# FFN by Strassen's products: operations behind a product spread over the next products, and one ring of PSUM banks for the up-projection

## The chip, the cores and the metric

The kernel runs on one core of a Trainium2 chip. The metric is the device time of one execution in microseconds (us), the median of several runs. The engines of the core are TensorE (PE, with its weight loads as PEld), VectorE (DVE), ScalarE (ACT), GpSimd (POOL) and SyncE (SP), which here only issues transfers. Each works through its own queue of instructions in order, and a wait at the head of a queue holds back everything behind it.

## The reference, cut to what matters

One layer of a decoder for a prompt of 2048 tokens and 8 samples of one token: a mixing part (a gated MLP group and an attention group), then the part that is changed here, a feed-forward network with a causal convolution over three tokens:

```python
def conv_ffn(x, conv_prev, g_ffn, w_up, w_conv, b_conv, w_down):
    h = rmsnorm(x, g_ffn)
    up = h @ w_up                        # 1024 -> 2 x 2816
    xp = jnp.concatenate([conv_prev, up], axis=1)
    c = b_conv
    for k in range(CONV_W):              # 3 taps over the tokens
        c = c + xp[:, k:k + T] * w_conv[k]
    gate, val = c[..., :D_FF], c[..., D_FF:]
    y = (jax.nn.silu(gate) * val) @ w_down
    return y, xp[:, -(CONV_W - 1):]
```

All of it is float32. A final rmsnorm over `x + y` gives the output.

## The kernel before, in words

Stages follow each other: projections, the gated MLP group, attention of the prompt, the output projection, and from about 1334 us on the FFN. Attention of the samples over their long cache is a generator (`sample_stream`); its steps are put between other matmuls by `fill(ns)`, which counts down the planned TensorE time, so they stand at fixed places of the order.

**Float32 matmuls.** Each operand is split into a high part (a rounded copy made by ACT) and a low part (the difference, made by POOL or DVE), and a product is three matmuls: high x high, high x low, low x high (`mm3`).

**The FFN.** Tokens go in four blocks of 512 (the last has 520 columns, samples included), each block in two halves of 256 (260). For every block, 22 units (`up`) follow, one for each group of 128 of the 2816 columns. A unit needs four results: gate and value, each for two halves of the tokens. It gets them with seven products instead of eight (Strassen's scheme), called P0 to P6 here, with the activations B11, T2, B21, T3, T1, T4, B22, in this order; the names stand in the rows as `up<-B11h` and so on. One product is 12 matmuls of 128x256. DVE adds the products up: `s` is a copy of P0 that ACT makes, `u` are partial sums, and gate first half = P2 + s, value first half = P5 + u, value second half = P4 + u, gate second half = P6 + u.

Behind each of the four results stands the convolution (`conv`): ACT puts the two last columns of the previous tokens in front (`up<-halo`), makes the third tap with the bias (`c<-up,gn`), and saves the new last columns (`halo<-up`); DVE adds two taps (`SCALAR_TENSOR_TENSOR c<-up,gn,c`). Then `glu`: ACT makes SiLU of the gate, DVE multiplies, ACT makes the high part (`gh`), DVE the low part (`gl`).

The down-projection goes in pairs of units: when both units of a pair have their `gh` and `gl`, eight pieces (six matmuls of 128x512 into a bank `d`, then an add of DVE to `y`) follow, spread over the next two units by the table `PIECES`. A unit has seven slots: slot j is product Pj and what follows it, `rest(j)`: loads, splits of weights, and the pieces of the table. In the last block a piece has two parts of 260 columns, and `late` (the final norm of the first three blocks) takes one step in each slot.

**Weights.** `split_w` makes the seven weight forms of a unit, one a slot, five products ahead, in six buffers `wu`: ACT the high part, POOL the low part. Forms 1, 4 and 6 come from two sums of DVE (`t<-vraw`, then `t<-t,graw`), made here at form 1. Forms 3 and 6 need a subtraction of POOL each, made at form 3. `vraw` is loaded in three buffers; the load of the half that the next unit's sums read waits until POOL is done with form 3 of the present one. The queue of SP issues these loads and the samples' cache pages (`cn`, `ct`) in one order. `split_d` makes the parts of the down weights (`wdh`, `wdl`).

**PSUM.** The products use single banks by name: "a" for P0 and P2, "b" for P1, P3 and P5, "c" for P4, "e" for P6; two banks `d` for the pieces. All of a unit's post-processing is put into the queues right behind the product that it belongs to:

```python
            copy(s1, prod(0, "a"))
            rest(0)
            dve.tensor_add(u2, s1, prod(1, "b"))
            rest(1)
            p = prod(2, "a")
            ...
            p = prod(6, "e")
            dve.tensor_add(p, u2, p)
            cg = conv(b, fi, 0, ps["e"], hm, hm)
            last = glu(cg, cv, gt, hm, hm)
            next(last)
            if not (b == NB - 1 and fi == NF - 1):
                run(last)
            rest(6)
```

At the end of a block `ending` computes the last pair's down-projection; `last_pieces` does so for the last block and overlaps it with the final norm.

Of the kernel before, what the change touches and what calls it, by code (L numbers as in the profile page):

```python
# [38 lines left out]
TA = 7  # L39
# [12 lines left out]
def build(tc, A):  # L52
# [1292 lines left out]
    PIECES = ((0, 0, 1, 1, 1, 0, 0), (1, 1, 1, 1, 1, 0, 0))  # L1345
# [30 lines left out]

    def split_w():
# [7 lines left out]
        A21, A22 = VAL[2 * q], VAL[2 * q + 1]  # L1385
        if j == 0:
            src = A11
        elif j == 1:
            TMP[1] = sb.tile([128, 4, 128], F32, tag="t1", bufs=1, name="t1")
            TMP[2] = sb.tile([128, 4, 128], F32, tag="t2", bufs=1, name="t2")  # L1390
            dve.tensor_add(TMP[1], A21, A22)
            dve.tensor_sub(TMP[2], TMP[1], A11)  # L1392
            src = TMP[2]
        elif j == 2:
            src = A12
        elif j == 3:
            pool.tensor_sub(A21, A11, A21)
            pool.tensor_sub(TMP[2], A12, TMP[2])
            src = A21
        else:  # L1400
            src = (TMP[1], A22, TMP[2])[j - 4]
        wts[i] = form(src)
# [165 lines left out]
    with ExitStack() as Fx:  # L1568
        one = mkpool(Fx, "f_1", 1)
        sb = mkpool(Fx, "f_s", 2)  # L1570
        pu = mkpool(Fx, "f_pu", 1, PSUM)
# [164 lines left out]
        def conv(b, fi, gv, p, o, m):  # L1736
            npr = min(m, max(0, SEQ - BL[b][0] - o))
            ix = gv * NF + fi
            w = [g(W_CONV, j * 2 * NF + ix) for j in range(3)]
            c = sb.tile([128, 260], F32, tag=f"c{gv}", bufs=2, name=f"c{gv}")  # L1740
            act.activation(p[:, 0:2], halo[:, ix, :], AF.Copy)  # L1741
            act.activation(c[:, 0:m], p[:, 2:2 + m], AF.Identity, scale=w[2], bias=g(B_CONV, ix))  # L1742
            act.activation(halo[:, ix, :], p[:, npr:npr + 2], AF.Copy)  # L1743
            for j in (1, 0):
                dve.scalar_tensor_tensor(out=c[:, 0:npr], in0=p[:, j:j + npr], scalar=w[j], in1=c[:, 0:npr], op0=ALU.mult, op1=ALU.add)  # L1745
            if m > npr:
                act.activation(state[:, ix, 2, :], p[:, 2 + npr:2 + m], AF.Copy)
                for j in range(2):
                    dve.scalar_tensor_tensor(out=c[:, npr:m], in0=state[:, ix, j, :], scalar=w[j], in1=c[:, npr:m], op0=ALU.mult, op1=ALU.add)  # L1749
            return c  # L1750

        def glu(cg, cv, gt, o, m):
            act.activation(cg[:, 0:m], cg[:, 0:m], AF.Silu)  # L1753
            dve.tensor_mul(cv[:, 0:m], cg[:, 0:m], cv[:, 0:m])  # L1754
            yield
            split_to(gt[0][:, o:o + m], gt[1][:, o:o + m], cv[:, 0:m])
# [5 lines left out]
        def pieces(b, fi, gts):  # L1762
            for m in range(8):
                w = wd(b, fi, m)
                for o, nn in parts(b):
# [12 lines left out]
        BANKS = ("d", "ua", "d", "ub", "ue", "uc")  # L1778
# [5 lines left out]
        def ending(b, gts):  # L1784
            ps = {}

            def part(m, j):
                w, gt = wd(b, NF - 2, m)(j), gts[j]
                mm3(ps[m], [(*w, gt[0][:, 0:512], gt[1][:, 0:512])], j == 0, j == 1)
                fill(3 * 512 / 2.4)  # L1790

            for i in (0, 1, 2, 3, 4, 8, 9, 5, 10, 11, 12, 13, 6, 14, 7, 15):
                m = i % 8
                if i < 8:
                    ps[m] = bank(m)
                    part(m, 0)
                    continue
# [49 lines left out]
        def last_pieces(gts):  # L1847
# [8 lines left out]
            def part(i, j):  # L1856
                o, nn, m = todo[i]
                w, gt = wd(b, NF - 2, m)(j), gts[j]
                mm3(ps[i][:, 0:nn], [(*w, gt[0][:, o:o + nn], gt[1][:, o:o + nn])], j == 0, j == 1)

            for i in range(16 + LAG):
                if i < 16:
                    ps[i] = bank(i)
                    part(i, 0)
                if i >= LAG:
# [80 lines left out]

        def up(b, fi, it, side, slow, hs):
            hm, H, q = BL[b][1], h2[b], b * NF + fi
            odd, ps = fi % 2, {}

            def prod(j, name):
                w, (xh, xl) = wts.pop(7 * q + j), H[FORMS[j]]
                ps[name] = p = pu.tile([128, 512], F32, tag="u" + name, name="up")
# [5 lines left out]
            def rest(j):  # L1959
                todo, later[:] = later[:], []  # L1960
# [19 lines left out]
            dve.tensor_add(u3, u2, prod(3, "b"))  # L1980
            rest(3)
            p = prod(4, "c")
            dve.tensor_add(u2, u2, p)
            dve.tensor_add(p, u3, p)
            rest(4)
            p = prod(5, "b")
            dve.tensor_add(p, u3, p)  # L1987
            cv = conv(b, fi, 1, ps["b"], 0, hm)
            if odd:
                take(it, 99)  # L1990
            gt = [sb.tile([128, 520], F32R, tag=t, bufs=3, name=t) for t in ("gh", "gl")]
            run(glu(cg, cv, gt, 0, hm))
            cv = conv(b, fi, 1, ps["c"], hm, hm)
            rest(5)
            p = prod(6, "e")
            dve.tensor_add(p, u2, p)
            cg = conv(b, fi, 0, ps["e"], hm, hm)
            last = glu(cg, cv, gt, hm, hm)
            next(last)
            if not (b == NB - 1 and fi == NF - 1):  # L2000
                run(last)
            rest(6)
            return gt, last
# [33 lines left out]
        for b in range(NB):  # L2037
# [4 lines left out]
            for fi in range(NF):  # L2042
# [5 lines left out]
                gt, last = up(b, fi, it, side, slow if fi else none, hs)  # L2048
# [5 lines left out]
                if fi % 2 == 0:  # L2054
                    before = gt
                elif fi < NF - 1:
                    it = pieces(b, fi - 1, (before, gt))
            split_d()
            if b < NB - 1:
                it = ending(b, (before, gt))  # L2060
# [6 lines left out]
                continue  # L2067
            sp.dma_start(out=A["o_pconv"], in_=halo)
            sp.dma_start(out=A["o_sconv"][:, :, 0, :], in_=state[:, :, 1, :])
            sp.dma_start(out=A["o_sconv"][:, :, 1, :], in_=state[:, :, 2, :])  # L2070
            split_d()
            assert next(slow, 0) == 0
            it = last_pieces((before, gt))
# [121 lines left out]
```

## Time and profile before

| | us |
|---|---|
| median of 3 runs (3658.9 to 3668.77) | 3663.0 |
| the profiled execution | 3664.04 |
| its span, first to last instruction | 3662.3 |
| mean granted TensorE clock over the span | 0.907 |
| PE, PEld, DVE, ACT, POOL busy, share of the span | 83%, 72%, 58%, 44%, 48% |

The span is what the trace covers; the execution takes 1.7 us more. A busy share is a mean over all stages. What a stage is bound by is seen in the rows on what each engine waits for, and in the order of time.

### The profile page before, as it was taken

The numbers are of one execution on the slowest core, as the hardware profiler recorded it, in microseconds if no ns is written. First come the engines' busy times: TensorE is split into PE (matmuls) and PEld (weight loads), VectorE is DVE, ScalarE is ACT, GpSimd is POOL, SyncE is SP. The second block draws the span as 40 slices with busy tenths as digits, with TensorE's granted clock in tenths as the row PEclk, the third lists the DMA queues.
The fourth block names the chain that finished last, engine by engine and source line by source line (L and its number), as shares of the span: only waits on it lengthen the run. The fifth ranks groups of instructions, "written<-read, shape, count | busy, mean of one in ns | idle before, by whom it ended". The sixth has DMA issues, their size and how long they took to land. (4 is left out here: it accounts for less than half of the span.)

```text
span 3662.3 us, 71440 instructions
## 1 busy us (share of the span) xinstructions
PE 3040.3 (83%) x24340; PEld 2651.6 (72%) x24340; DVE 2120.6 (58%) x4367; ACT 1627.3 (44%) x4025; POOL 1770.5 (48%) x1665
## 2 busy tenths in 40 slices
PE   8998999999999967878778877777888885767676
PEld 7897887888778966767767776666676764767676
DVE  6564226777774455555565455566555556666565
ACT  4333336777872234433334344444344434444444
POOL 3332223223324555555555555556566655555554
PEclk9999999999999988989888898888999987878888
DMA  5448667887578965646666663476666533233232
GB/s 169 132 154 256 173 182 213 219 228 189 137 195 236 247 191 167 196 148 201 187 196 213 190 200 106 121 216 188 185 191 189 172 98 117 87 104 101 87 108 47
DMA packets 410760, 616.63 MB, mean 168 GB/s; under 512 B 69855, under 2 KB 300926, under 8 KB 410398
## 3 DMA queue, kind: packets, MB, share of 16 engines
q1 hardware_dynamic: 372560, 518.56, 47.8%
q0 software_dynamic: 26480, 87.14, 8.7%
q10 hardware_dynamic: 11358, 6.36, 0.6%
q8 instruction: 195, 3.19, 0.4%
q14 instruction: 167, 1.37, 0.1%
HBM read 547.58 MB, written 64.28 MB: 167 GB/s over the span
## 5 line engine op out<-in xcount | busy, mean ns | idle before, releaser
L126 POOL TENSOR_TENSOR wu<-t,wu 128x512 fp32r<-128x512 f32 x264 | 345.4, 1308 | 510.5 <-ACT wu L86 486.2
L1745 DVE SCALAR_TENSOR_TENSOR c<-up,gn,c 128x256 f32<-128x256 f32 (+2 forms) x704 | 340.7, 484 | 372.5 <-ACT halo L1743 359.9
L76 PE MATMUL up<-B21h,wu 128*128 128x256 f32 (+1 forms) x704 | 211.0, 376 | 366.5 <-ACT s L86 366.5
L76 PEld LDWEIGHTS up<-B21h,wu 128*128 128x128 f32 x704 | 165.2, 270 | 390.1 <-ACT s L86 386.7
L76 PE MATMUL dp<-gh,wdh 128*128 128x512 f32 (+1 forms) x800 | 305.4, 382 | 70.4 <-DVE y L1769 69.9
L126 POOL TENSOR_TENSOR wdl<-draw,wdh 128x512 fp32r<-128x512 f32 x171 | 228.6, 1337 | 254.9 <-ACT wdh L86 249.3
L86 ACT ACTIVATE wu<-t 128x512 fp32r<-128x512 f32 x264 | 164.1, 622 | 358.0 <-DVE t L1392 355.2
L76 PE MATMUL dp<-gl,wdh 128*128 128x512 f32 (+1 forms) x800 | 299.4, 374 | 0.0
L76 PE MATMUL dp<-gh,wdl 128*128 128x512 f32 (+1 forms) x800 | 297.2, 371 | 0.0
L126 POOL TENSOR_TENSOR wu<-vraw,wu 128x512 fp32r<-128x512 f32 x176 | 229.8, 1306 | 116.5 <-ACT wu L86 116.5
L126 POOL TENSOR_TENSOR wu<-graw,wu 128x512 fp32r<-128x512 f32 x176 | 228.2, 1297 | 103.6 <-ACT wu L86 103.6
L1741 ACT ACTIVATE up<-halo 128x2 f32<-128x2 f32 x352 | 59.3, 169 | 477.2 <-DVE up L1987 217.1
L1769 DVE TENSOR_TENSOR y<-y,dp 128x512 f32<-128x512 f32 (+1 forms) x400 | 226.6, 577 | 59.4 <-PE dp L76 58.5
L76 PE MATMUL s<-k,q 96*128 96x512 f32 (+2 forms) x960 | 254.1, 376 | 6.5 <-DVE S L1203 2.5
L76 PEld LDWEIGHTS dp<-gh,wdh 128*128 128x128 f32 x800 | 168.8, 211 | 88.7 <-DVE y L1769 74.0
L126 DVE TENSOR_TENSOR pl<-t,ph 128x512 fp32r<-128x512 f32 (+1 forms) x320 | 194.0, 606 | 53.0 <-ACT ph L86 49.4
L86 ACT ACTIVATE ph<-t 128x512 fp32r<-128x512 f32 (+1 forms) x320 | 170.2, 532 | 107.1 <-PE t L1227 102.8
L1215 ACT ACTIVATE S<-S,nm 128x512 f32<-128x512 f32 (+2 forms) x320 | 207.9, 650 | 5.7 <-POOL nm L1207 5.7
L1742 ACT ACTIVATE c<-up,gn 128x256 f32<-128x256 f32 (+1 forms) x352 | 199.3, 566 | 11.7
L76 PEld LDWEIGHTS s<-k,q 96*128 96x128 f32 x960 | 170.3, 192 | 45.2 <-DVE S L1203 10.1
L76 PEld LDWEIGHTS dp<-gh,wdl 128*128 128x128 f32 x800 | 166.5, 208 | 23.9
L76 PEld LDWEIGHTS dp<-gl,wdh 128*128 128x128 f32 x800 | 168.2, 210 | 11.7
(460 smaller groups left out, 9145.5 us busy)
## 6 DMA issues: line engine op xcount, KB each, us to landing
ct<-in_cT SPq DMA_DIRECT2D x1024, 144.0 KB
cn<-in_cN SPq DMA_DIRECT2D x1024, 128.0 KB
draw<-in_w_down SPq DMA_DIRECT2D x176, 256.0 KB
vraw<-in_w_up SPq DMA_DIRECT2D x174, 256.0 KB
graw<-in_w_up SPq DMA_DIRECT2D x87, 512.0 KB
q_sp<-qs SPq DMA_DIRECT2D x48, 256.0 KB
ft<-x_sp SPq DMA_DIRECT2D x48, 256.0 KB
xt<-in_xT SPq DMA_DIRECT2D x16, 512.0 KB
```

Of the source, the lines that this page charges most:

```text
L76: pe.matmul(out, lhsT=w, rhs=x, start=start, stop=stop)
L86: act.activation(out, in_, AF.Copy)
L126: (lo_eng or dve).tensor_sub(lo, src, f(hi))
L1215: act.activation(s, s, AF.Exp, scale=SCALE, bias=d["nm"][:, qb:qb + 1], accum_out=d["ls"][:, qb, r:r + 1])
L1741: act.activation(p[:, 0:2], halo[:, ix, :], AF.Copy)
L1742: act.activation(c[:, 0:m], p[:, 2:2 + m], AF.Identity, scale=w[2], bias=g(B_CONV, ix))
L1745: dve.scalar_tensor_tensor(out=c[:, 0:npr], in0=p[:, j:j + npr], scalar=w[j], in1=c[:, 0:npr], op0=ALU.mult, op1=ALU.add)
L1769: dve.tensor_add(y, y, p[:, 0:nn])
```

## The change

Five things change, all in the FFN. No operation is added or removed: every engine keeps its number of instructions.

- A table `defer` holds operations by slot, and `flush()` at the head of `rest` puts those of the present slot into the queues. The third tap and the halo copies (`conv_init`), the two taps of DVE (`taps`), SiLU, the product, `gh` and `gl` of one result now stand in different slots, up to slot 11 of the unit, that is slot 4 of the next one.
- The products' banks turn in one ring of four (`pu`, tag "u"); the bank of P5 is taken before that of P4.
- `PIECES` of the even unit is (0, 0, 0, 0, 1, 1, 1) and no longer (0, 0, 1, 1, 1, 0, 0).
- DVE's two sums for the weights are made one slot earlier (behind form 0), POOL's two subtractions too (behind form 2).
- `ending` and `last_pieces` call `flush()` for the operations that the last unit has left over, and the two stores of the convolution's state come four steps later.

```diff
-    PIECES = ((0, 0, 1, 1, 1, 0, 0), (1, 1, 1, 1, 1, 0, 0))
+    PIECES = ((0, 0, 0, 0, 1, 1, 1), (1, 1, 1, 1, 1, 0, 0))
...
+    def sums(A11, A21, A22):
+        for i in (1, 2):
+            TMP[i] = sb.tile([128, 4, 128], F32, tag=f"t{i}", bufs=1, name=f"t{i}")
+        dve.tensor_add(TMP[1], A21, A22)
+        dve.tensor_sub(TMP[2], TMP[1], A11)
...
+        wts[i] = form(src)
+        if j == 0 and not i:
+            return
         if j == 0:
...
+            sums(A11, A21, A22)
+        if j == 2:
             pool.tensor_sub(A21, A11, A21)
             pool.tensor_sub(TMP[2], A12, TMP[2])
...
-        pu = mkpool(Fx, "f_pu", 1, PSUM)
+        pu = mkpool(Fx, "f_pu", 4, PSUM)
...
+        def flush():
+            for fn in defer.pop(pos["t"], ()):
+                fn()
+            pos["t"] += 1
...
-            copy(s1, prod(0, "a"))
+            copy(s1, prod(0))
             rest(0)
-            dve.tensor_add(u2, s1, prod(1, "b"))
+            add(u2, s1, prod(1))
             rest(1)
-            p = prod(2, "a")
-            dve.tensor_add(p, s1, p)
-            cg = conv(b, fi, 0, ps["a"], 0, hm)
+            p = prod(2)
+            add(p, s1, p)
+            at_slot(2, lambda: init(0, 0, 2))
+            at_slot(3, lambda: tap(0, 0, 2))
             rest(2)
...
+            at_slot(5, lambda: silu(0), lambda: init(1, 0, 5))
+            at_slot(6, lambda: init(1, 1, 4), lambda: tap(1, 0, 5), lambda: tap(1, 1, 4))
+            rest(5)
+            p3 = prod(6)
+            at_slot(7, lambda: add(p3, u2, p3), lambda: init(0, 1, 6), lambda: gmul(0))
+            at_slot(8, lambda: ghi(0), lambda: tap(0, 1, 6))
+            at_slot(9, lambda: glo(0), lambda: silu(1))
+            at_slot(10, lambda: gmul(1), lambda: ghi(1))
+            at_slot(11, lambda: glo(1))
+            rest(6)
```

ACT's queue around the end of an odd unit in the second block, before. The first three rows belong to P6; `c<-c` is SiLU, `gh` the high part of the gated result, `wu` a weight form, and `s` the copy of the next unit's P0:

```order
L1741 ACTIVATE up<-halo 128x2
L1742 ACTIVATE c_26883<-up,gn 128x256
L1743 ACTIVATE halo<-up 128x2
L1753 ACTIVATE c_26883<-c_26883 128x256
L86 ACTIVATE gh<-c_26854 128x256
L86 ACTIVATE wu<-t_26785 128x512
L86 ACTIVATE s_26898<-up 128x256
L86 ACTIVATE wu<-vraw 128x512
```

The same place in the changed kernel:

```order
L1747 ACTIVATE up<-halo 128x2
L1748 ACTIVATE c_26869<-up,gn 128x256
L1749 ACTIVATE halo<-up 128x2
L86 ACTIVATE wu<-t_26754 128x512
L86 ACTIVATE s_26882<-up 128x256
L1747 ACTIVATE up<-halo 128x2
L1748 ACTIVATE c_26994<-up,gn 128x256
L1749 ACTIVATE halo<-up 128x2
L86 ACTIVATE wu<-vraw 128x512
L86 ACTIVATE gh<-c_26845 128x256
L86 ACTIVATE wu<-t_26755 128x512
L2010 ACTIVATE c_26994<-c_26994 128x256
```

SiLU (L1753, now L2010) and `gh` stood ahead of the copy `s` and now stand behind it; the halo copies of P6 stood ahead of it too and are now the rows right behind it.

DVE's queue in the even unit that follows, from P1's add to P4's, before (`t<-vraw` and `t<-t,graw` are the sums for the weights, `y` the add of a piece):

```order
L1974 TENSOR_TENSOR u_26899<-s_26898,up 128x256
L1977 TENSOR_TENSOR up<-s_26898,up 128x256
L1745 SCALAR_TENSOR_TENSOR c_27047<-up,gn,c_27047 128x256 x2
L1769 TENSOR_TENSOR y_26005<-y_26005,dp 128x512
L1980 TENSOR_TENSOR u_26900<-u_26899,up 128x256
L1391 TENSOR_TENSOR t_27080<-vraw 128x512
L1392 TENSOR_TENSOR t_27081<-t_27080,graw 128x512
L1769 TENSOR_TENSOR y_26007<-y_26007,dp 128x512
L1983 TENSOR_TENSOR u_26899<-u_26899,up 128x256
```

The same place in the changed kernel, up to the first piece's add:

```order
L2026 TENSOR_TENSOR u_26883<-s_26882,up 128x256
L1757 SCALAR_TENSOR_TENSOR c_26994<-up,gn,c_26994 128x256 x2
L2026 TENSOR_TENSOR up<-s_26882,up 128x256
L2023 TENSOR_TENSOR gl<-c_26845,gh 128x256
L1380 TENSOR_TENSOR t_27053<-vraw 128x512
L1381 TENSOR_TENSOR t_27054<-t_27053,graw 128x512
L2026 TENSOR_TENSOR u_26884<-u_26883,up 128x256
L2014 TENSOR_TENSOR c_26869<-c_26994,c_26869 128x256
L1757 SCALAR_TENSOR_TENSOR c_27044<-up,gn,c_27044 128x256 x2
L2026 TENSOR_TENSOR u_26883<-u_26883,up 128x256
L2026 TENSOR_TENSOR up<-u_26884,up 128x256
L2023 TENSOR_TENSOR gl<-c_26869,gh 128x256
```

The sums stood behind the add of P3 and now stand ahead of it, behind the add of P2; the rest of the previous unit's gate and product (taps, `gl`, `c<-c,c`, the second `gl`) stands among this unit's adds, and no piece comes before P4.

## Rows read from the trace of the kernel before

**Rows 1.** The page: busy shares, and the granted clock in 40 slices.
```profile
PE 3040.3 (83%) x24340; PEld 2651.6 (72%) x24340; DVE 2120.6 (58%) x4367; ACT 1627.3 (44%) x4025; POOL 1770.5 (48%) x1665
PEclk9999999999999988989888898888999987878888
```

**Rows 2.** Stretches (units 2 to 19): length; PE, PEld, DVE, ACT, POOL busy; clock; DMA; GB/s.
```profile
1392.00:1837.00 445.00, 364.32 (x3208) 319.02 (x3208) 234.69 (x479) 178.06 (x484) 252.80 (x200) 0.90 0.61 182
1961.00:2408.00 447.00, 358.98 (x3164) 318.40 (x3163) 237.64 (x491) 187.86 (x496) 250.39 (x199) 0.89 0.55 162
2529.00:2953.00 424.00, 354.09 (x2714) 298.62 (x2712) 236.94 (x456) 178.94 (x489) 254.69 (x205) 0.92 0.60 176
3093.00:3575.00 482.00, 334.01 (x2390) 325.25 (x2389) 297.65 (x643) 204.66 (x540) 272.07 (x208) 0.83 0.30 97
```

**Rows 3.** TensorE's waits from 1334 to 3640: total us, times, longest.
```profile
PE up L76 <- ACT s L86: 366.5, 73, 11.7
PE dp L76 <- DVE y L1769: 69.9, 20, 7.6
```

**Rows 4.** TensorE in time, an even unit: start, us, operation, idle time before.
```profile
2633.58 0.58 PE L76 MATMUL up<-B21h,wu 128*128 128x256 f32 x1 [7.54 <-ACT s L86]
...
2638.01 0.40 PE L76 MATMUL dp<-gl,wdh 128*128 128x512 f32 x1
```

**Rows 5.** ACT in time, the same stretch.
```profile
2628.98 0.63 ACT L86 ACTIVATE wu<-vraw 128x512 fp32r<-128x512 f32 x1 [2.60 <-POOL vraw L1397]
2629.52 0.16 ACT L1741 ACTIVATE up<-halo 128x2 f32<-128x2 f32 x1
...
2632.32 0.42 ACT L86 ACTIVATE gh<-c 128x256 fp32r<-128x256 f32 x1 [0.49 <-DVE c L1754]
2633.16 0.36 ACT L86 ACTIVATE s<-up 128x256 f32<-128x256 f32 x1
```

**Rows 6.** TensorE in time at full clock: P0, a piece, P1, a sample step.
```profile
2649.00 0.28 PE L76 MATMUL up<-B11h,wu 128*128 128x256 f32 x1
...
2650.42 0.40 PE L76 MATMUL dp<-gh,wdh 128*128 128x512 f32 x1
...
2651.80 0.28 PE L76 MATMUL up<-T2h,wu 128*128 128x256 f32 x1
...
2657.30 0.38 PE L76 MATMUL up<-B21h,wu 128*128 128x256 f32 x1 [0.41 <-ACT s L86]
```

**Rows 7.** Sample steps of TensorE (tile po), busy us in the third block.
```profile
2529.00:2953.00 424.00, 42.09 (x704) 17.09 (x704) 1.92 (x4) 0.92 0.60 176
```

**Rows 8.** DVE in time: an add and the taps behind it, and two prices of the sums.
```profile
2647.78 0.43 DVE L1987 TENSOR_TENSOR up<-u,up 128x256 f32<-128x256 f32 x1 [0.74 <-PE up L76]
2649.11 1.01 DVE L1745 SCALAR_TENSOR_TENSOR c<-up,gn,c 128x256 f32<-128x256 f32 x2 [0.90 <-ACT halo L1743]
...
2662.26 1.65 DVE L1391 TENSOR_TENSOR t<-vraw 128x512 f32<-128x512 f32 x1
2663.99 1.60 DVE L1392 TENSOR_TENSOR t<-t,graw 128x512 f32<-128x512 f32 x1
```

**Rows 9.** DVE by form in the second block: busy, mean ns, idle before.
```profile
L1391 DVE TENSOR_TENSOR t<-vraw 128x512 f32<-128x512 f32 x18 | 16.5, 918 | 11.8 <-DMA vraw<-in_w_up 9.0 <-POOL wdl L126 2.9
L1392 DVE TENSOR_TENSOR t<-t,graw 128x512 f32<-128x512 f32 x18 | 14.3, 795 | 1.6
```

**Rows 10.** The page: the low parts that POOL makes.
```profile
L126 POOL TENSOR_TENSOR wu<-t,wu 128x512 fp32r<-128x512 f32 x264 | 345.4, 1308 | 510.5 <-ACT wu L86 486.2
```

**Rows 11.** SP's queue in time: page loads of the samples, weight loads.
```profile
2216.58 9.33 SPq L66 DMA_DIRECT2D cn<-in_cN  x16
...
2226.48 0.86 SPq L66 DMA_DIRECT2D vraw<-in_w_up  x2
```

**Rows 12.** DVE in time, behind those loads.
```profile
2230.44 0.69 DVE L1391 TENSOR_TENSOR t<-vraw 128x512 f32<-128x512 f32 x1 [2.48 <-DMA vraw<-in_w_up]
```

**Rows 13.** The same view: units 0 and 1 of the second block.
```profile
1925.00:1962.00 37.00, 29.21 (x314) 27.96 (x315) 20.52 (x39) 16.01 (x41) 23.80 (x19) 0.87 0.76 246
```

More of the change, by code (lines that the diff above doesn't have):

```diff
@@ L1385, in split_w @@
         A21, A22 = VAL[2 * q], VAL[2 * q + 1]
-        if j == 0:
[L1387 to L1396, printed above, removed]
+        if j in (0, 2):
+            src = (A11, A12)[j // 2]
+        elif j == 1:
+            if not q:
+                sums(A11, A21, A22)
+            src = TMP[2]
+        else:
+            src = (A21, TMP[1], A22, TMP[2])[j - 3]
+        wts[i] = form(src)
+        if j == 0 and not i:
+            return
+        if j == 0:
+            sums(A11, A21, A22)
+        if j == 2:
             pool.tensor_sub(A21, A11, A21)
             pool.tensor_sub(TMP[2], A12, TMP[2])
[L1399 to L1402, printed above, removed]
         if j == 4:
@@ L1764, in pieces @@
                 w = wd(b, fi, m)
+                if m == 0:
+                    gts = [G[i] for i in gts]
                 for o, nn in parts(b):
@@ L1973, in up, with ghi, glo, add @@
+            def ghi(h):
+                if not h:
+                    G[q] = [sb.tile([128, 520], F32R, tag=t, bufs=3, name=t) for t in ("gh", "gl")]
+                copy(G[q][0][:, h * hm:h * hm + hm], c[1, h][:, 0:hm])
+            def glo(h):
+                o = slice(h * hm, h * hm + hm)
+                dve.tensor_sub(G[q][1][:, o], c[1, h][:, 0:hm], f(G[q][0][:, o]))
+            def add(out, a, p):
+                dve.tensor_add(out, a, p)
+            copy(s1, prod(0))
             rest(0)
-            dve.tensor_add(u2, s1, prod(1, "b"))
+            add(u2, s1, prod(1))
@@ L1985, in up @@
+            add(u2, u2, p)
+            add(p, u3, p)
             rest(4)
-            p = prod(5, "b")
-            dve.tensor_add(p, u3, p)
-            cv = conv(b, fi, 1, ps["b"], 0, hm)
+            p = prod(5)
+            add(p, u3, p)
+            at_slot(5, lambda: silu(0), lambda: init(1, 0, 5))
[3 more added lines that the diff above has]
+            at_slot(7, lambda: add(p3, u2, p3), lambda: init(0, 1, 6), lambda: gmul(0))
@@ L1996, in up @@
[L1996 to L2003, printed above, removed]
         def last_stat():
@@ L2047, in build @@
                     hs = load_h2(b + 1)
-                gt, last = up(b, fi, it, side, slow if fi else none, hs)
+                up(b, fi, it, side, slow if fi else none, hs)
                 if b == 0 and fi == 0:
@@ L2053, in build @@
                     take(load_y(b), 99)
[L2054 to L2057, printed above, removed]
+                last2 = b * NF + fi - 1, b * NF + fi
+                if fi % 2:
+                    it = pieces(b, fi - 1, last2) if fi < NF - 1 else none
             split_d()
             if b < NB - 1:
-                it = ending(b, (before, gt))
+                it = ending(b, last2)
                 for _ in range(8):
@@ L2067, in build @@
                 continue
+            split_d()
+            assert next(slow, 0) == 0
+            it = last_pieces(last2)
+            act.activation(sb.tile([128, 1], F32, tag="tw", bufs=1, name="tw"), epst, AF.Sqrt)
+            take(it, 4)
             sp.dma_start(out=A["o_pconv"], in_=halo)
@@ L2070, in build @@
             sp.dma_start(out=A["o_sconv"][:, :, 1, :], in_=state[:, :, 2, :])
-            split_d()
-            assert next(slow, 0) == 0
-            it = last_pieces((before, gt))
-            act.activation(sb.tile([128, 1], F32, tag="tw", bufs=1, name="tw"), epst, AF.Sqrt)
-            take(it, int(T6))
-            run(last)
-            take(it, int(TA))
+            take(it, int(T6) + int(TA) - 4)
             r0 = root(0)
```

72 lines of the change are left out of this document (44 added, 28 removed).

## The prediction, written before the changed kernel ran

> **What bounds the kernel now.** The page first: TensorE is busy 83% of the span, and its granted clock falls in the second half [rows 1]. Then the busy times by stretch, for the FFN: in units 2 to 19 of a block (nine pairs of units) TensorE is busy 364 of 445, 359 of 447, 354 of 424 and 334 of 482 us, and no other engine comes near its limit, POOL with 250 to 272 us and DVE with 235 to 298 [rows 2]. So an order of waits bounds it. TensorE's own waits name it: 366.5 us in 73 waits for ACT's copy `s`, and 69.9 us for DVE's adds of pieces [rows 3].
>
> How such a wait comes about stands in time. TensorE stops for 7.54 us before P2 of an even unit and then runs at 1.2 GHz until about 2638.0 [rows 4]. P2 goes into the bank that P0 left, and P0 waits there for the copy `s`. ACT makes it last: it is held 2.60 us by POOL's subtraction for a weight form, then come the halo copies, SiLU and `gh` of the unit before, each waiting for DVE, and `s` starts only at 2633.16 [rows 5]. At full clock TensorE needs far less: a product takes 1.42 us (2649.00 to 2650.42), a piece 1.38 (2650.42 to 2651.80) [rows 6]. A pair of units is 14 products and 8 pieces, 19.9 + 11.0 = 30.9 us; sample steps add 42.1 / 9 = 4.7 [rows 7]: 35.6 us, against (445 + 447 + 424) / 27 = 48.7 now. In the last block it is 31.6 (260 columns, no samples), against 482 / 9 = 53.6.
>
> **The change, part by part.** Counts stay, so everything is a matter of waits.
>
> *The copy `s` and the ring.* `s` no longer stands behind SiLU and `gh`, and P2 takes a bank that P4 left. The 7.5 us wait goes. What is late next? I go through an even unit of the changed kernel, from t = 0, the end of P5 of the odd unit before; until P4 of the even unit no piece stands in TensorE's way, so alone it would end P6 at 1.4, P0 at 2.8, P1 at 4.3, P2 at 5.7. The taps of P5 start 1.35 us after its end (add at 2647.78, taps at 2649.11) and take 1.0 [rows 8]. ACT then has two weight copies (0.54 from start to start [rows 5]), to 2.4, and the halo copies of P4 (0.85, what the 1.35 leave beside the add), to 3.25; DVE takes its taps to 4.3, then P6's add to 4.75, ACT P6's halo copies to 5.6, DVE P6's taps to 6.7. P3 needs that bank: 1.0 us late.
>
> *The sums a slot earlier.* They can't start before `vraw` has landed, and that load waits for POOL's low part of form 3. Its copy on ACT comes behind P5's halo copies and a down weight, at about 2.4, and POOL does the down weight and the form one after the other at 1.3 us each [rows 10], to about 4.5. From issue to use the one measured wait gives 3.1 us (issued by 2227.34, sums at 2230.44) [rows 11, 12]; with the issue 0.4: 8.1. The two sums cost 0.92 + 0.80 = 1.7 [rows 9], to 9.8. Behind them in DVE's queue stand P3's add, the product, two taps, P4's two adds and the second `gl`: five operations of 0.43 and a pair of taps of 1.0 [rows 8], 3.2, so `gl` is there at 13.0. The first piece stands behind P4, which ends at 9.6 with the 1.0 above; four of its matmuls (0.9) need nothing new, the fifth needs `gl`: 13.0 − 10.5 = 2.5 us wait. So an even unit still waits 1.0 + 2.5 = 3.5 us.
>
> *What comes on top or off.* A sample step stands in such a run more often than not and covers part: −0.9 (bounds 0 and −1.9). SP's queue: 16 page loads hold the weight loads 9.33 us [rows 11], and a load so held lands late by up to that; today 11.8 + 1.6 = 13.4 us of idle time at these sums in 18 units are all it costs [rows 9], since the sums come a slot later. Bounds 0 and 9.3 for an even unit; I take 1.6, since only some units are hit and most hits are short. An idle stretch can bring half speed: after 0.41 us none (a full-speed row, 0.38) [rows 6], after 7.54 us 4.4 us of it, a loss of 2.2 [rows 4]; for 2 to 4 us I take 1.7. Odd units have a piece behind each of five products and so twice the time for the same chains; bounds 0 and 3, I take 1.0. The pair: 35.6 + 3.5 − 0.9 + 1.6 + 1.7 + 1.0 = 42.5 us, and 27 x (48.7 − 42.5) = 167 us gained in three blocks.
>
> The rows of DVE show the sums at 0.69 us [rows 12] and at 1.65 and 1.60 us [rows 8]. The Trainium skill (GPSIMD Engine Reference, "Key points", and SBUF — State Buffer, "SBUF: two separate sides") says that GpSimd and a DVE operation with two SBUF inputs take one shared port in turn, each for a whole instruction. By that rule a POOL that works closer to the sums, as it will, makes the dear price the usual one: 3.25 for 1.7, and over 36 even units some 56 us less gained, 3411 us. The slow rows agree with it; the means of rows 9 lie between, and the sum goes by these.
>
> *The last block.* There DVE is busy 298 us in nine pairs, 33.1 a pair [rows 2], more than TensorE's 31.6, because of the final norm of the earlier blocks. DVE keeps waits that the change does not touch (0.9 us before each of the eight pairs of taps [rows 8], in part filled): 33.1 + 9 = 42 (bounds 36 and 50). Gain: 9 x (53.6 − 42) = 104 us.
>
> *Units without pieces* (0 and 1 of each block) take 37 us now [rows 13]. TensorE needs 2 x 9.9, POOL 2 x 9 x 1.3 = 23.4; with 6 us for the start of a block 29.5: 4 x 7 = 28 us. Unit 20 and the products of 21: 3 us in each block, 12. The end of a block keeps its work, with the leftovers in its queues: 0 (bounds −8 and 8 each). POOL's two subtractions a slot earlier free ACT of its 2.60 us wait, which is inside the above.
>
> The sum: 167 + 104 + 28 + 12 = 311, and 3664 − 311 = 3353; the profiled execution is 1 us above the median of three, so I say **3355 us**.
>
> **The rivals.** *Nearly all idle time goes* (14%): loads land in time and sample steps cover the rest. For it: no engine but TensorE has more to do in a pair than POOL's 254.7 / 9 = 28.3 us [rows 2]. Against it: the chain through `vraw` above. Pairs of 38 and 36 us: 27 x 10.7 + 9 x 17.6 + 28 + 20 = 495, 3169 us.
>
> *The sums at the head of DVE's queue take the place of the copy* (17%). Both units of a pair wait for `vraw` or for POOL, and DVE holds taps and adds behind it. For it: the idle time of these sums already names `vraw` and POOL [rows 9]. Against it: odd units have twice the time. Pairs of 47 and 48: 27 x 1.7 + 9 x 5.6 = 96, 3568 us.
>
> *No gain that can be measured* (3%): the deferred operations run in the old order in effect, since each queue waits at the same products. The rows of the order speak against it.
>
> *Slower* (6%): the page loads. With pairs 15% shorter the 16-fold bursts stand ahead of the weight loads more often; if every even unit gets `vraw` a whole burst late, the pair is 35.6 + 3.5 + 9.3 + 2.2 + 1.0 = 51.6, and with the last block as now 27 x 2.9 = 78 more: 3742 us. It decides from a mean delay of about 6.5 us on. Against it: a longer pair gives the queue its time back.
>
> **How the numbers follow.** The forecast has 60%, with a range of its own of 3280 to 3440. With half of the first rival and most of the second, 3190 to 3570 holds eight times in ten. Faster by over 0.3% (about what a measurement of this kernel can tell from no change): 0.60 + 0.14 + 0.17 = 0.91; the same 0.03; slower 0.06.
>
> **What the profile after would show.** Right: the wait of products for `s` under 60 us in all; new waits of P3 for DVE's taps and of `dp` for `gl` in even units, 1 to 4 us each; sums that wait for `vraw` in most even units; a granted clock of 0.93 or more in units 2 to 19 of the first three blocks; DVE the engine next to its limit in the last. Wrong: products that wait for `wu` (the weights bound it), waits of sample matmuls for their pages, or odd units with waits as long as the even ones.

## The result, and the profile after

The changed kernel takes 3551.9 us (median of three runs, 3551.3 to 3557.0) against 3663.0; the ratio is 0.970, 95% interval 0.967 to 0.972. It is faster by 111 us; the forecast was 308 us, 3355. The page of the changed kernel, answering to [rows 1]:

```profile
PE 3040.0 (86%) x24340; PEld 2625.1 (74%) x24340; DVE 2178.8 (61%) x4367; ACT 1609.0 (45%) x4029; POOL 1792.2 (50%) x1665
PEclk9999999999999998889988898997898988889988
```

TensorE has the same work, and the clock still falls in the second half. ACT has four instructions more than before (4029 against 4025): four more loads of its function tables, 1.28 us each. Units 2 to 19 of the four blocks, changed kernel, columns as in [rows 2]:

```profile
1380.10:1821.90 441.80, 365.58 (x3207) 314.62 (x3206) 242.39 (x482) 173.60 (x481) 256.66 (x199) 0.90 0.62 184
1944.00:2380.60 436.60, 355.49 (x3159) 312.00 (x3158) 248.26 (x495) 185.86 (x499) 260.22 (x201) 0.90 0.54 162
2509.10:2938.00 428.90, 359.76 (x2711) 297.45 (x2709) 239.85 (x460) 175.53 (x490) 261.23 (x207) 0.91 0.60 174
3057.80:3467.60 409.80, 329.41 (x2384) 313.25 (x2384) 332.55 (x645) 197.91 (x541) 276.32 (x209) 0.89 0.35 114
```

The first three blocks, for which 167 us were forecast, gained 8 (445 + 447 + 424 to 442 + 437 + 429); the last gained 72 (482 to 410). By the starts of the first products in both traces, units 0 and 1 of the four blocks went from 168 to 183 us (lost 15), unit 20 from 126 to 113, unit 21 with the end of the block from 238 to 206 (gained 32), and the FFN starts 3 us earlier: 8 + 72 − 15 + 13 + 32 + 3 = 113, against 112 us between the spans.

TensorE's waits in the changed kernel from 1334 to 3540, answering to [rows 3] (total us, times, longest):

```profile
PE dp L76 <- ACT gh L86: 178.6, 42, 14.0
PE dp L76 <- DVE gl L2023: 84.2, 49, 3.8
PE up L76 <- DVE u L2026: 40.0, 15, 7.9
PE dp L76 <- DVE y L1775: 31.7, 26, 4.5
PE up L76 <- ACT s L86: 19.3, 18, 3.0
PE up L76 <- DVE c L1757: 14.7, 12, 3.7
...
PE lp L76 <- ACT wd L86: 0.7, 1, 0.7
```

The wait for `s` is gone, from 366.5 us to 19.3. In its place the first piece waits for `gh` and `gl`. DVE's waits at the weight sums, same stretch, say why:

```profile
DVE t L1380 <- DMA vraw<-in_w_up: 142.9, 24, 10.4
DVE t L1380 <- issue: 75.0, 15, 12.6
DVE t L1380 <- POOL wu L126: 8.4, 4, 3.0
```

The kernel before had 32.5, 9.8 and, on POOL, 2.9 us there. For a wait marked `issue` the trace shows no releaser; these go with the load, since they fall to 1.4 us when it is issued earlier (below). One even unit of the second block shows the whole chain. SP's queue in the changed kernel (start, us, operation):

```profile
1988.67 6.80 SPq L66 DMA_DIRECT2D draw<-in_w_down  x3
1996.07 10.60 SPq L66 DMA_DIRECT2D ct<-in_cT  x16
...
2007.55 0.81 SPq L66 DMA_DIRECT2D vraw<-in_w_up  x2
```

POOL, in the same stretch, was done with the low part of form 3, for which the load waits, at 1996.3:

```profile
1995.04 1.27 POOL L126 TENSOR_TENSOR wu<-vraw,wu 128x512 fp32r<-128x512 f32 x1
```

The load's buffer was free at 1996.3, and the load went at 2007.5, behind sixteen pages of the samples. DVE, from the first `gl` on:

```profile
1999.33 0.42 DVE L2023 TENSOR_TENSOR gl<-c,gh 128x256 fp32r<-128x256 f32 x1
2012.38 0.69 DVE L1380 TENSOR_TENSOR t<-vraw 128x512 f32<-128x512 f32 x1 [12.64 <-issue]
2013.18 0.69 DVE L1381 TENSOR_TENSOR t<-t,graw 128x512 f32<-128x512 f32 x1
2013.79 0.42 DVE L2026 TENSOR_TENSOR u<-u,up 128x256 f32<-128x256 f32 x1
2014.12 0.42 DVE L2014 TENSOR_TENSOR c<-c,c 128x256 f32<-128x256 f32 x1
...
2016.03 1.11 DVE L2023 TENSOR_TENSOR gl<-c,gh 128x256 fp32r<-128x256 f32 x1
```

Behind the sums stand P3's add, the product `c` (from which ACT makes `gh`) and the second `gl`. TensorE, at the first piece:

```profile
2015.04 0.79 PE L76 MATMUL dp<-gh,wdh 128*128 128x512 f32 x1 [14.03 <-ACT gh L86]
2017.19 0.80 PE L76 MATMUL dp<-gl,wdh 128*128 128x512 f32 x1 [1.36 <-DVE gl L2023]
...
2021.62 0.57 PE L76 MATMUL dp<-gh,wdl 128*128 128x512 f32 x1
2022.03 0.39 PE L76 MATMUL dp<-gh,wdh 128*128 128x512 f32 x1
```

It stands for 14.03 us, and its matmuls then take 0.79 us in place of 0.39 (1.2 in place of 2.4 GHz; the granted clock from 2015 to 2022 is 0.50) until about 2022.0.

### The profile page after: what moved, and what is told of

Read it like the earlier page. It is cut to its first block, busy times and chain, and to the rows that moved or that the text cites. A ratio compares the mean times of both kernels' runs of the same rounds, so it can differ in the third digit from the quotient of the medians.

```text
span 3550.1 us, 71345 instructions
## 1 busy us (share of the span) xinstructions
PE 3040.0 (86%) x24340; PEld 2625.1 (74%) x24340; DVE 2178.8 (61%) x4367; ACT 1609.0 (45%) x4029; POOL 1792.2 (50%) x1665
## 5 line engine op out<-in xcount | busy, mean ns | idle before, releaser
L76 PE MATMUL dp<-gh,wdh 128*128 128x512 f32 (+1 forms) x800 | 306.4, 383 | 210.7 <-ACT gh L86 178.6
L126 POOL TENSOR_TENSOR wu<-t,wu 128x512 fp32r<-128x512 f32 x264 | 353.7, 1340 | 211.0 <-ACT wu L86 211.0
L126 POOL TENSOR_TENSOR wu<-graw,wu 128x512 fp32r<-128x512 f32 x176 | 244.9, 1392 | 130.4 <-ACT wu L86 120.5
L86 ACT ACTIVATE gh<-c 128x256 fp32r<-128x256 f32 (+1 forms) x176 | 73.5, 418 | 376.3 <-DVE c L2014 376.3
L126 DVE TENSOR_TENSOR pl<-t,ph 128x512 fp32r<-128x512 f32 (+1 forms) x320 | 193.9, 606 | 53.1 <-ACT ph L86 49.4
L1380 DVE TENSOR_TENSOR t<-vraw 128x512 f32<-128x512 f32 x88 | 72.0, 818 | 227.5 <-DMA vraw<-in_w_up 142.9
L76 PE MATMUL up<-T4h,wu 128*128 128x256 f32 (+1 forms) x704 | 182.5, 337 | 1.4 <-DVE u L2026 1.2
```

Source lines behind the costliest of these rows:

```text
L76: pe.matmul(out, lhsT=w, rhs=x, start=start, stop=stop)
L86: act.activation(out, in_, AF.Copy)
L126: (lo_eng or dve).tensor_sub(lo, src, f(hi))
```

## The experiments

Times are medians of four runs (the changed kernel's of three), each with its ratio to runs of the kernel before on the same chip, whose medians lay between 3661 and 3665 us. The last two columns are the length of a pair of units in units 2 to 19 (by the starts of the products in each trace): mean of the first three blocks, and the last.

| | us | ratio, 95% interval | pair | last block |
|---|---|---|---|---|
| before | 3663 | | 48.7 | 53.5 |
| changed | 3551.9 | 0.970 (0.967 to 0.972) | 48.4 | 45.5 |
| ring alone | 3517.9 | 0.961 (0.959 to 0.962) | 44.4 | 53.7 |
| ring, earlier sums | 3574.7 | 0.976 (0.974 to 0.978) | 45.2 | 57.6 |
| changed, banks by name | 3562.2 | 0.973 (0.971 to 0.974) | 48.3 | 45.1 |
| changed, sums back a slot | 3537.8 | 0.967 (0.964 to 0.969) | 46.7 | 50.3 |
| changed, no sums | 3301.5 | 0.902 (0.901 to 0.904) | 41.9 | 43.5 |
| changed, vraw issued by POOL | 3509.7 | 0.959 (0.957 to 0.961) | 46.5 | 48.0 |
| changed, vraw earlier on SP | 3445.6 | 0.940 (0.938 to 0.943) | 45.3 | 46.8 |
| sums behind gl | 3401.4 | 0.929 (0.926 to 0.932) | 43.8 | 47.0 |
| sums behind gl, vraw by POOL | 3474.1 | 0.948 (0.946 to 0.951) | 45.4 | 49.0 |
| sums behind gl, vraw earlier on SP | 3377.7 | 0.922 (0.919 to 0.924) | 42.7 | 48.0 |
| sums behind gl, later pieces | 3414.6 | 0.932 (0.929 to 0.935) | 43.8 | 47.7 |
| changed, no norm in the last block | 3522.2 | 0.961 (0.958 to 0.964) | 48.5 | 42.1 |
| ring alone, vraw earlier on SP | 3551.9 | 0.969 (0.967 to 0.971) | 45.4 | 55.4 |
| before, vraw earlier on SP | 3683.5 | 1.006 (1.003 to 1.008) | 49.4 | 54.2 |

**The loads of vraw issued by POOL.** The load stands behind form 3 in POOL's own queue:

```diff
-            sp.dma_start(out=t, in_=A["w_up"]...)
+            gq.dma_start(out=t, in_=A["w_up"]...)
...
+        if j in (3, 5) and q:
+            load_v()
         if j == 4:
             later.append(load_g)
-            if q:
-                later.append(load_v)
...
```

> The changed kernel, with the loads of the halves vraw issued by POOL right behind the forms that free their buffers, so that nothing on SP stands in front of them. Theory A (the waits of the even units' first piece come from vraw landing late behind SP's bursts of sample pages): DVE's wait at the first sum for vraw and for its issue, 218 us in the changed kernel, falls under 70; the wait of dp for gh and gl, 263 us, falls by 80 to 130, pairs of the first three blocks from 48.4 to about 44.5, time 3430 (3400 to 3470). Rival B (the chain of DVE and ACT operations behind P4 to P6 is too long by itself, as the last block shows, where the sums hardly wait and dp waits as long): the wait for vraw goes, dp's wait stays above 220, time 3520 to 3560.

Measured: 3509.7 us, between the two. The first sum's waits for `vraw`, POOL and the issue fell from 227 to 40 us, but each sum took longer (1207 and 832 ns on average; in the changed kernel 818 and 809), and the wait for `gh` only fell to 133.7. The experiment changes two things, the time of the load and POOL's work, so it decided nothing by itself.

**No sums.**

```diff
-        dve.tensor_add(TMP[1], A21, A22)
-        dve.tensor_sub(TMP[2], TMP[1], A11)
...
-            src = TMP[2]
+            src = A11
...
-            src = (A21, TMP[1], A22, TMP[2])[j - 3]
+            src = (A21, A22, A22, TMP[2])[j - 3]
...
-            pool.tensor_sub(TMP[2], A12, TMP[2])
+            pool.tensor_sub(TMP[2], A12, A22)
```

> The changed kernel without DVE's two sums for the weights (forms 1 and 4 are made from halves as loaded, form 6 from a difference of two loaded halves, so the products are of other numbers); DVE never waits for vraw. Theory A (late vraw holds DVE): dp's wait for gh and gl from 263 to under 140, time 3400 (3360 to 3440). Rival B (the chain itself): only 1.7 us of sums leave the chain of each unit, dp's wait stays above 180, time 3480 to 3530.

Measured: 3301.5 us, 250 less than the changed kernel. The wait for `gh` falls to 28.9 us, with `gl` 113 in all, as theory A had it; the time is 100 us below its 3400. So the largest part of the loss comes with the sums: their waits, their own time and their place together. The pair is still 41.9 us, hardly less than the 42.5 that the forecast gave it with the sums.

**The ring apart from the deferral.** Banks by name in the changed kernel:

```diff
-                ps[j] = pu.tile([128, 512], F32, tag="u", name="up")
+                ps[j] = pu.tile([128, 512], F32, tag="u" + "ababcbe"[j], name="up")
...
```

> The changed kernel with the products' banks by name again (a for P0 and P2, b for P1, P3, P5, c for P4, e for P6) in place of the ring; everything else as changed. Theory (the deferral takes SiLU and gh from in front of the copy s, the ring only removes what is left of the wait for s): P2 waits 1 to 2 us for s in even units, time 3570 to 3610. Rival (the ring is what removes the wait): the wait for s stays above 200 us in all and the time above 3630.

Measured: 3562.2 us, 10 more than with the ring, a little under the range; P2's wait for `s` is 19.8 us in all. And the ring in the kernel before:

```diff
-        pu = mkpool(Fx, "f_pu", 1, PSUM)
+        pu = mkpool(Fx, "f_pu", 4, PSUM)
...
-                ps[name] = p = pu.tile([128, 512], F32, tag="u" + name, name="up")
+                if name == "b" and j == 5:
+                    ps["b"] = ps.pop("f")
+                else:
+                    if j == 4:
+                        ps["f"] = pu.tile([128, 512], F32, tag="u", name="up")
+                    ps[name] = pu.tile([128, 512], F32, tag="u", name="up")
+                p = ps[name]
```

> The kernel before with the ring of four banks for the products in place of the named ones, nothing deferred, its table of pieces and its place of the sums kept. If the ring carries the gain: P2 no longer waits for s, the late copy only holds P4 and P5 two slots later, the wait for s falls from 366 to under 150 us, time 3560 to 3600. If the deferral carries it: the wait only moves to a later product, TensorE loses as much, time 3630 to 3670.

Measured: 3517.9 us, below both ranges: the ring alone is 34 us faster than the whole change. TensorE's waits with the ring alone, same stretch:

```profile
PE dp L76 <- ACT gh L86: 128.1, 36, 5.9
PE dp L76 <- DVE y L1769: 111.6, 38, 7.1
PE up L76 <- DVE c L1745: 63.6, 38, 5.2
PE lp L76 <- ACT wd L86: 25.6, 4, 8.7
```

No wait for `s` is among the large ones (1.0 us in all). So either part alone, the ring or the deferral, takes that wait away. In the first three blocks the ring alone gives 44.4 us a pair and the whole change 48.4; in the last block 53.7 and 45.5. What was added to the ring costs 4.0 us a pair in the first three blocks, where the samples' pages are loaded, and brings 8.2 in the last, which has no pages, but also other pieces and the norm.

**The place of the sums.** First back at the slot where they stood before:

```diff
-        if j == 0:
-            sums(A11, A21, A22)
-        if j == 2:
+        if j == 3:
             pool.tensor_sub(A21, A11, A21)
```

(form 1 calls `sums` again.)

> The changed kernel with the sums and the two subtractions at the slot where the kernel before had them (form 1 and form 3); ring, deferral and table of pieces as changed. Theory C (what costs the gain is that the sums, with their wait for vraw, stand in DVE's queue ahead of the product and the low part that the even unit's first piece needs): the sums now stand behind the product, so gh is no longer held, only the second gl is; dp's wait for ACT gh falls from 179 to under 90, time 3490 (3460 to 3515). Rival D (the deferral and the late start of the pieces themselves cost it): dp's wait stays above 220, time 3535 to 3565.

Measured: 3537.8 us, in the range of theory D; but the wait for `gh` went to 18.8 us as theory C had it, and others rose: `gl` to 145.5, since the sums now stand right ahead of the second one, and `s` from 19.3 to 87.5. ACT now waits for the sums and for POOL's subtraction:

```profile
ACT wu L86 <- DVE t L1381: 219.8, 80, 10.3
ACT wu L86 <- POOL vraw L1400: 123.1, 51, 4.2
```

In the changed kernel these two are 29.3 and 24.4 us. So the earlier sums free ACT's queue and load DVE's. That ACT's wait makes `s` late is not shown: with the sums behind `gl` (below) ACT waits 330.8 us for them, and `s` costs 31.2. Theory C is borne out for `gh` and not for the time. The earlier sums without the deferral:

```diff
...
+        if j == 0:
+            sums(A11, A21, A22)
+        if j == 2:
             pool.tensor_sub(A21, A11, A21)
             pool.tensor_sub(TMP[2], A12, TMP[2])
```

> The kernel before with the ring, and with the sums and subtractions a slot earlier as in the change; no deferral, its table of pieces. Ring alone took 3518. Theory C: the earlier sums wait for vraw in this order as well, and by them alone it loses what separates the ring alone from the whole change, 30 to 50 us, time 3540 to 3570. Rival D (the loss belongs to the deferral with its table of pieces): the earlier sums cost little here, time 3505 to 3530.

Measured: 3574.7 us, just above theory C's range and 57 more than the ring alone, most of it in the last block, and 0.7 us a pair in the first three. So the earlier sums do cost in this order too, though not where the whole change loses. Then the sums two slots later, behind the second `gl`:

```diff
         q, j = divmod(i, 7)
+        j = (0, 2, 1, 3, 4, 5, 6)[j]
...
+            sums(A11, A21, A22)
             src = TMP[2]
...
-        wts[i] = form(src)
+        wts[7 * q + j] = form(src)
...
-        if j == 0:
-            sums(A11, A21, A22)
-        if j == 2:
+        if j == 1:
             pool.tensor_sub(A21, A11, A21)
```

> The changed kernel with the forms of a unit made in the order 0, 2, 1, 3 to 6, and the sums at form 1, so that they stand behind the second gl in DVE's queue, two slots later than in the change; the subtractions follow behind form 1. Theory C: dp's wait for gh and gl, 263 us, falls under 130, DVE's wait for vraw under 60, pairs of the first three blocks to 43 to 44, time 3430 (3390 to 3470). Rival: the later form 1 makes products wait for wu, or the wait moves to the adds of the pieces behind the sums; time 3490 or more.

Measured: 3401.4 us, 150 less than the changed kernel, inside the range of theory C. TensorE's and DVE's waits in it:

```profile
PE dp L76 <- DVE gl L2019: 78.1, 49, 3.3
...
PE dp L76 <- ACT gh L86: 29.6, 30, 4.4
```

```profile
DVE t L1380 <- DMA vraw<-in_w_up: 35.0, 12, 5.5
DVE t L1380 <- issue: 27.9, 6, 8.4
```

**The load earlier in SP's queue.** The loads stay on SP and are put right behind the forms that free their buffers:

```diff
+        if j in (3, 5) and q:
+            load_v()
         if j == 4:
             later.append(load_g)
-            if q:
-                later.append(load_v)
-        if j == 6:
-            if q:
-                later.append(load_v)
-            else:
-                later.append(load_g)
+        if j == 6 and not q:
+            later.append(load_g)
```

> The changed kernel with the loads of vraw put into SP's queue right behind forms 3 and 5, nearly one to two slots earlier, so that fewer page loads and loads of down weights stand ahead of them; nothing else moves. Theory C with the queue's delay as its size (the sums' place makes the wait matter, SP's queue makes it long): DVE's wait at the sums for vraw and its issue, 218 us in the changed kernel, falls under 120, time 3500 (3480 to 3525), near the 3510 that the loads issued by POOL gave. Rival (the queue's delay is not what costs; the kernel with the loads on POOL won by something else): 3540 to 3565.

Measured: 3445.6 us, 106 less than the changed kernel, twice what was expected. The same even unit as above, SP's queue:

```profile
1960.51 0.34 SPq L66 DMA_DIRECT2D vraw<-in_w_up  x1
...
1961.92 9.55 SPq L66 DMA_DIRECT2D ct<-in_cT  x16
```

The load now goes ahead of the pages. POOL and DVE there, around the sums:

```profile
1963.52 1.56 POOL L126 TENSOR_TENSOR wu<-t,wu 128x512 fp32r<-128x512 f32 x1
1965.05 1.70 POOL L126 TENSOR_TENSOR wu<-graw,wu 128x512 fp32r<-128x512 f32 x1
```

```profile
1963.50 0.42 DVE L2020 TENSOR_TENSOR gl<-c,gh 128x256 fp32r<-128x256 f32 x1
1963.96 1.67 DVE L1380 TENSOR_TENSOR t<-vraw 128x512 f32<-128x512 f32 x1
1965.72 1.58 DVE L1381 TENSOR_TENSOR t<-t,graw 128x512 f32<-128x512 f32 x1
```

The sums follow `gl` without a wait, and TensorE waits 3.29 us, no longer 14.03:

```profile
1968.47 0.50 PE L76 MATMUL dp<-gh,wdh 128*128 128x512 f32 x1 [3.29 <-ACT gh L86]
1970.61 0.79 PE L76 MATMUL dp<-gl,wdh 128*128 128x512 f32 x1 [1.65 <-DVE gl L2020]
```

The same edit in three other kernels. With the sums behind `gl`:

> The kernel with the sums behind the second gl (3401), with the loads of vraw earlier in SP's queue in the same way. If vraw's landing no longer matters once the sums stand behind gl: 3390 to 3410. If the 63 us that its sums still wait cost as much as they last: 3350 to 3380. Slower than 3415 if SP, now waiting for POOL at these loads, holds pages or down weights.

Measured: 3377.7 us, 24 less than without it and inside the second range; the first sum's wait is 3.3 us. It is the fastest kernel that does all the work, 8% faster than before. With the loads issued by POOL in that kernel:

> As the kernel with the sums behind the second gl, and the loads of vraw issued by POOL behind forms 3 and 5. If two slots later are enough for vraw to land (theory C), this changes the time by under 15 us; if loads held on SP still cost there, it is 20 to 50 us faster than that kernel.

Measured: 3474.1 us, 73 slower, against both expectations, though the sums have no wait for `vraw` left. POOL's own issues, by form:

```profile
L66 POOL DMA_DIRECT2D vraw<-in_w_up x171 | 95.2, 557 | 53.4 <-POOL wu L126 42.4 <-PE up L76 3.9 <-PE dp L76 3.5
```

With the ring alone, and with nothing else in the kernel before:

> The ring alone (3518), with the loads of vraw put into SP's queue right behind forms 3 and 5; no deferral, sums at form 1. If the delay on SP costs only where the sums stand ahead of gl: 3495 to 3520. If any order of DVE's queue pays for it: 3440 to 3475, no slower than the whole change with the same edit (3446).

> The kernel before, with nothing but the loads of vraw put into SP's queue right behind forms 3 and 5. There the products wait for the copy s, not for the sums (13 us of waits for vraw in units 2 to 19 of the first three blocks' rows). If the delay on SP became a cost only by the change: 3640 to 3670. If it was one already: 3560 to 3630.

Measured: 3551.9 and 3683.5 us, slower by 34 and by 19 than without the edit, and above every range named. So the earlier load, worth 106 us in the changed kernel, gives nothing back in the order before. Why it costs there is not settled: the waits of the sums for `vraw` go (1.0 us in all with the ring), the sums get longer (1281 and 1004 ns on average, 1117 and 902 with the ring alone), and SP waits 724 us for POOL's `wu` at the head of its queue, 249 with the ring alone. That wait rises as much where the edit helps (149 to 559 us in the changed kernel), so it isn't the reason by itself. A cost of the edit may also hide a gain from the shorter delay; no run separates the two.

**Two trials of what is left.** The first piece a slot later, with the sums behind `gl`:

```diff
-    PIECES = ((0, 0, 0, 0, 1, 1, 1), (1, 1, 1, 1, 1, 0, 0))
+    PIECES = ((0, 0, 0, 0, 0, 1, 1), (2, 1, 1, 1, 1, 0, 0))
```

> The kernel with the sums behind the second gl, and the table of pieces (0,0,0,0,0,1,1), (2,1,1,1,1,0,0): the first piece of a pair one slot later. If the even unit's first piece is still held by gl and gh (108 us there): that wait goes, time 3330 to 3375. If the chain of DVE and the banks sets the pace, the wait moves to the products (up waiting for DVE's c and for s) and the time stays at 3390 to 3420.

Measured: 3414.6 us, 13 slower. The waits for `gh` and `gl` fall from 108 to 53 us, and those for the adds `y` rise from 28 to 85. The products' waits hardly change (`c` 58.6 to 60.4, `s` 31.2 to 37.6), so the time is as the second expectation had it, but the wait moved to the pieces' adds and not to the products. And the changed kernel without the norm in its last block:

```diff
-                slow = late()
+                slow = none
```

> The changed kernel without the final norm of the first three blocks inside the last block (their part of the output is left out). If DVE's work for that norm is what keeps the last block's pair at 45.5 us: the pair falls to 37 to 40, time 3485 (3470 to 3505). If the chain of an even unit (taps, gl) does: the pair stays at 43 to 45, time 3530 to 3550.

Measured: 3522.2 us, the last block's pair 42.1: between the two expectations. The norm makes 3.4 us of the 45.5, about a quarter of what lies above the full-clock 31.6. The same stretch as the last row of the four above:

```profile
3060.00:3439.30 379.30, 318.05 (x2378) 306.58 (x2378) 296.87 (x597) 174.39 (x508) 257.11 (x201) 0.91 0.23 75
```

## Why the prediction was wrong, point by point

**The step that failed** is the wait at the even unit's first piece. The walk gave it 2.5 us, and the term for SP's queue put 1.6 on top: "Bounds 0 and 9.3 for an even unit; I take 1.6, since only some units are hit and most hits are short". Together that is 4.1 us a pair; in units 2 to 19 of the first three blocks TensorE waited there 6.8 us, 143.6 in all for `gh` and 40.2 for `gl`. SP's term was sized by the idle time at the sums in the kernel before [rows 9], where they stand a slot later, and so it took over the slack that the change removes. In the changed kernel the first sums wait 227 us, 218 of them in 39 waits for the load or its issue, and what stands behind them on DVE is what the first piece needs. Taking most of that delay away (`vraw` earlier on SP) gave 106 us: 85 in units 2 to 19 of the first three blocks, which is 3.1 us a pair where the term had 1.6; 26 in units 0 and 1; and less than nothing in the last block (11 lost). In the kernel before the same edit gave nothing.

**The walk itself** was short by more than SP's term. With the load early the pair is 45.3 us; the forecast without its term for SP would be 42.5 − 1.6 = 40.9. Means over the even units 2 to 18 of the first three blocks, in us from the start of P6, by the times of the traces:

| | walk | changed | vraw earlier on SP |
|---|---|---|---|
| form 3's low part ends | 4.5 | 6.9 | 6.7 |
| the first sum starts | 8.1 | 14.4 | 12.0 |
| the second sum ends | 9.8 | 16.3 | 14.2 |
| P4 ends | 9.6 | 11.5 | 11.6 |
| TensorE's waits at the pieces of the unit | 2.5 | 6.8 | 4.8 |

SP's delay is 2.4 of the 6.3 us by which the sums are late; the rest is there without it. With the sums behind `gl` and the load early the wait at the pieces is 2.4 us and the pair 42.7. One part of the lateness: in the unit above ACT, ahead of form 3's copy, waits for a down weight that SP loads:

```profile
1993.10 0.63 ACT L86 ACTIVATE wdh<-draw 128x512 fp32r<-128x512 f32 x1 [4.00 <-DMA draw<-in_w_down]
1993.63 0.62 ACT L86 ACTIVATE wu<-vraw 128x512 fp32r<-128x512 f32 x1
```

The walk had followed SP's queue only for `vraw`, not for the loads that ACT stands behind.

**TensorE's own time** was short too. The forecast's 42.5 us are 37.3 of work (35.6, and 1.7 for half speed) and 5.2 of waits; by the trace a pair is 40.0 us busy and 8.4 idle (before: 39.9 and 8.8). The 4.7 us for sample steps count one kind of them (tile `po`) in the third block [rows 7]; all that TensorE does in a pair beside products and pieces was busy 6.0 us, before and after. The 1.4 us of busy time that are left go with a clock lower than forecast; no run separates them.

**The second rival**, the sums at the head of DVE's queue in the place of the copy, given 17%, is what happened in the first three blocks: a pair of 48.4 where it gave 47. Its 3568 us lie 16 from the time. For the last block it gave 48, and 45.5 was measured. That odd units wait as well it had wrong: there the pieces wait 17.7 us for `y` in the 27 pairs, in the even ones 183.8 for `gh` and `gl`.

**The copy `s`**: right, 19.3 us are left, under the 60 named. Of the two new waits one came: `gl` costs 1.7 us on average. P3's wait for taps, 1.0 us in the walk, did not: the 14.7 us in which products wait for `c` stand at P1 and P2. Not named was the largest wait, 178.6 us for `gh`, whose product stands behind the sums too. But the forecast gave the gain to the deferral and the ring together, and the ring alone brings all of the measured gain and more in the first three blocks.

**Units 0 and 1**: 28 us forecast as a gain, 15 lost. P6 waits there for `u` (33.3 of the 40.0 us above, in 8 waits), which stands behind sums that wait for `vraw`. With the load early the four blocks' units 0 and 1 come to 157 us, 11 better than before.

**The last block**: 72 of 104 us, a pair inside its bounds. The mechanism was right, no wait for `s` and DVE the engine next to its limit; DVE was undersized: 332.6 us in nine pairs, 36.9 each, where the forecast took over 33.1 from the kernel before. The growth lies in one kind of operation, the 72 taps on the samples' eight columns. Before, then changed:

```profile
L1749 DVE SCALAR_TENSOR_TENSOR c<-state,gn,c 128x8 f32<-128x8 f32 x72 | 16.0, 223 | 1.3
L1760 DVE SCALAR_TENSOR_TENSOR c<-state,gn,c 128x8 f32<-128x8 f32 x72 | 60.1, 835 | 1.3
```

They take 44 us more (the first sum gives 8 back, 1109 to 680 ns). It comes with the deferral: 222 ns with the ring alone, 845 with banks by name. In the changed kernel 53 of the 72 last over 400 ns, and each of these ends 0.02 to 0.03 us after an operation of POOL does; before, 64 of the 72 ran with POOL idle. The 9 us of waits on top were more than the eight times 0.9 that the forecast names for them; 8.6 came.

**Unit 20**: 13 us for 12. **The ends**: 32 us for 0 (bounds 8 each). In the kernel before, the products at the end of a block waited for a down weight that ACT makes:

```profile
PE lp L76 <- ACT wd L86: 24.9, 4, 8.1
```

In the changed kernel this is 0.7 us, with the ring alone still 25.6. So the deferral takes that wait away: the last unit's operations no longer stand in front of that copy. The ring takes another, of the next block's P0 for a bank that an add to `y` frees: 22.2 us before, 1.7 with the ring alone, 23.7 with banks by name.

**The port.** The sums at 0.69 us in the one unit and at 1.67 and 1.58 in the other, beside POOL's low parts, differ as in [rows 8, 12]. The Trainium skill (GPSIMD Engine Reference, "Key points") says that GpSimd shares its SBUF interfaces with DVE, and that they contend when a DVE instruction has two SBUF inputs; the second unit agrees with it, 3.25 us for two sums. In the changed kernel the means are 818 and 809 ns, near the 1.7 us of the forecast: 65 of the 88 first sums ran with POOL idle, at about 0.69 us, and 23 beside it, at 1.19. The taps of the last block paid instead.

**The clock**: 0.93 or more was named for the first three blocks; it was 0.90, 0.90 and 0.91, as long waits remained. With the sums behind `gl` and the load early it is 0.97, 0.97 and 0.95:

```profile
1389.00:1771.60 382.60, 348.64 (x3206) 301.56 (x3206) 248.65 (x481) 175.82 (x479) 254.05 (x198) 0.97 0.72 212
1878.00:2260.10 382.10, 342.67 (x3159) 301.97 (x3159) 254.54 (x491) 188.74 (x501) 256.08 (x200) 0.97 0.65 192
2362.60:2750.10 387.50, 351.76 (x2711) 290.64 (x2709) 251.57 (x468) 177.72 (x490) 258.72 (x205) 0.95 0.70 203
```

What stays open: why the last block gets slower in every changed kernel in which the sums or their load are moved (45.5 to between 46.8 and 50.3), and why the earlier load costs in the order before.

## What to carry to other kernels

An operation that waits for a load is cheap at the end of an engine's queue and dear in front of work that the bounding engine needs; when a change moves it forward, its wait has to be priced at the new place, not by the idle time that the old place shows. Look at everything that stands ahead of the load in the queue that issues it, and ahead of the operation that frees its buffer. A change of several parts should be timed part by part: here the ring alone was faster than the whole, and the rest was worth having only with the sums or their load moved.

## What the hardware showed that was not expected

POOL as the issuer of 171 loads was busy 95 us with them (557 ns each), and the two kernels with it were 64 and 96 us slower than the same order with SP as issuer (3509.7 against 3445.6, 3474.1 against 3377.7); the issues are at most a part of that, and no run shows the rest. In the first of them the first sum took 1207 ns on average, with SP as the issuer 829.

A DVE operation on eight columns took 223 ns on average in one order and 835 in another, and each long one ended with an operation of POOL. A short operation of DVE that a change moves is to be priced by what POOL does beside it.
